# A convolution tile of the larger token group placed ahead of the first pointwise output projection on TensorE, and the value weights stored 128 bytes further on

## The chip, the core and the metric

The kernel runs on one core of one Trainium2 chip. The metric is the device time of one execution in microseconds (us), the median of several runs; lower is better. In the profile PE is TensorE (PEld its weight loads), DVE is VectorE, ACT is ScalarE, POOL is GpSimd and SP is the engine that issues the DMAs. Each engine takes its instructions in the order in which they stand in the program.

## What is computed

One step of a two-layer streaming encoder over 640 tokens (512 of a prompt, 8 streams of 16 new frames) with 1024 features, all in float32. Layer 0 is a convolution module, layer 1 is attention over a shared K/V; each is followed by a SwiGLU feed-forward net (FFN) with 2816 hidden features.

```python
def conv_module(h, hist, g, w_pw1, b_pw1, w_dw, b_dw, ln_g, ln_b, w_pw2, b_pw2):
    a, gate = jnp.split(rms_norm(h, g) @ w_pw1 + b_pw1, 2, axis=-1)
    glu = a * jax.nn.sigmoid(gate)
    full = jnp.concatenate([hist.astype(glu.dtype), glu], axis=1)
    y = lax.conv_general_dilated(full, w_dw[:, None, :], ...) + b_dw   # causal, per feature, width 31
    y = jax.nn.silu(layer_norm(y, ln_g, ln_b))
    return h + y @ w_pw2 + b_pw2, full[:, -CONV_HIST:]

h = swiglu_ffn(h, norm_ffn[l], w_ffn_in[l], w_ffn_out[l])          # after each layer
k, v = jnp.split(rms_norm(h, norm_kv) @ w_kv, 2, axis=-1)          # once, for layer 1
```

## The kernel before, in words

Features lie on the 128 partitions in 8 chunks (c = 0 to 7), tokens along the free dimension. The tokens are cut in two groups: group 0 has 256, group 1, the larger, has 384.

**Products.** Each float32 product is made of three matmuls on split operands: a weight tile `raw` is loaded by SP, ACT copies its high part to `whi` (line 156), and DVE, POOL or both write the rest to `wlo` (line 160; with `pool=3` DVE does the first quarter of the columns and POOL the other three). `whi` and `wlo` have two buffers each, so the weights after next can be split only when PE has made its last matmul with the older ones. Activations are split in the same way into `x` (high part by ACT, line 165, low part by DVE, line 166). Lines 176 to 178 are the three matmuls: high times high, low weight times high, high weight times low activation.

**The first stage.** The string `PLAN` lists its steps in program order, each with a group and chunks. Those that matter here:

- `b7`, `b5`, `b6`: the pointwise input projection (`pw1`) of chunk 7, 5 or 6 for group 1, 48 matmuls of 384 columns, then the gate (ACT lines 386 and 389, DVE line 401), which fills the chunk's row of `gp`.
- the depthwise convolution of a chunk is done on one of three engines. `d145` does chunks 4 and 5 of group 1 on DVE (lines 440 and 443, one instruction per tap and chunk); `q16` does one on ACT and POOL; `l13` and `p13` do chunk 3 of group 1 on PE. `l13` loads: POOL builds the diagonal weights (`w`, line 450) and SP copies the chunk to DRAM and back in four shifted pieces (`sc` and `x`, lines 458 and 461). `p13` is 32 matmuls (line 475; a profile shows each as two records), and ACT writes the result to `y` (line 477).
- `n0`, `n1`: the layer norm of the convolution's result. Sums by POOL (`acc`, line 201) and PE (line 210), DVE and POOL make the factor (lines 232 and 236), PE spreads it over the partitions (line 222), DVE multiplies (line 495), ACT applies the Silu (line 497), and the result is split into `x`.
- `w0`: the pointwise output projection (`pw2`) of group 0, with four weights, two outputs of 24 matmuls each; DVE adds each output to `h` (line 512).
- `r0`: the RMS norm ahead of the FFN for group 0: squares by ACT, sums by POOL and PE (line 210), factor (lines 232 and 236), spread (line 222), DVE multiplies (line 249), and a split into `x`.
- `f`: a part of the FFN of group 0. Each of its first six weights (f0 to f5 below) gives two outputs (48 matmuls of 256 columns), then follow the output weights.

The instructions are not run in plain program order: a scheduler lays them out for each engine by priority and by when it expects their inputs (splits of weights and the gates come with a raised priority, DVE's convolution fills in between), and this order is then fixed.

**The attention stage.** `proj_v` makes the values. There the split weights are the moving operand of 256 columns and the activations the stationary one: 4 weight tiles, 5 token tiles each, 24 matmuls per token tile, 480 in all.

Of the kernel before, what the change touches and what calls it, by code (L numbers as in the profile page):

```python
# [9 lines left out]
F32R = mybir.dt.float32r  # L10
# [58 lines left out]
FIN = ((4, 0), (3, 0), (2, 0), (4, 1), (1, 0), (3, 1), (0, 0), (2, 1), (1, 1), (0, 1))  # L69
SSQ1 = 'ppapappp'  # L70
LNO = ((1, 5, 4, 3, 6, 0, 2, 7), (3, 5, 6, 4, 2, 7, 1, 0))
PLAN = ("a0 y a1 a2 a4 x a3 a5 a6 l04 p04 l05 d0213 a7 b0 p05 b1 l07 p07 l06 b2 q00 s0 p06 n0 b3 b4 b5 d145 l13 w0 b7 r0 p13 b6 f q16 s1 d101 d127 n1 f f w1 r1")

V_NCONV, V_BPW1, V_BDW, V_LNG, V_LNB, V_BPW2 = 0, 8, 24, 32, 40, 48
V_NKV, V_NATT, V_NFFN, V_NFIN, V_N = 56, 64, 72, 88, 96
# [4 lines left out]
def tile_trunk(ctx, tc, xT, vecs, hist, w_pw1, w_pw2, w_in0, w_out0, w_in1, w_out1,  # L80
# [48 lines left out]
    def col(base, i):  # L129
        return vec[:, base + i:base + i + 1]  # L130

    def wsplit(src, k, n, parts=1, pool=0, cuts=1, gains=None):
        third[0] += 1
        pool3, tag = (third[1], "rx") if third[1] and third[0] % 3 == 0 else (wp, "raw")
        raw = pool3.tile([P, 2048], F32, tag=tag, name=nm(tag))
        hi = wp.tile([P, 2048], F32R, tag="whi", name=nm("whi"))
        lo = wp.tile([P, 2048], F32R, tag="wlo", name=nm("wlo"))
        sz = k * n
        if parts > 1:
            nc.sync.dma_start(raw[:, :sz].rearrange("p (m c) -> p m c", m=parts), src)  # L140
        else:
            src = src if len(src.shape) == 2 else src.rearrange("p m c -> p (m c)")
            for i in range(cuts):
                a, b = sz * i // cuts, sz * (i + 1) // cuts
                nc.sync.dma_start(raw[:, a:b], src[:, a:b])
        if gains is not None:
            for a, b, gain in gains:
                nc.scalar.activation(out=hi[:, a:b], in_=raw[:, a:b], func=AF.Copy, scale=gain)
                nc.vector.scalar_tensor_tensor(out=lo[:, a:b], in0=raw[:, a:b], scalar=gain,
                                               in1=hi[:, a:b].bitcast(F32), op0=ALU.mult,  # L150
                                               op1=ALU.subtract)
            return hi, lo
        with tc.high_priority(offset=HP):
            for i in range(cuts):
                a, b = sz * i // cuts, sz * (i + 1) // cuts
                nc.scalar.activation(out=hi[:, a:b], in_=raw[:, a:b], func=AF.Copy)  # L156
                c = b - (b - a) * pool // 4
                for eng, a, b in ((nc.vector, a, c), (nc.gpsimd, c, b)):
                    if a < b:
                        eng.tensor_tensor(out=lo[:, a:b], in0=raw[:, a:b],  # L160
                                          in1=hi[:, a:b].bitcast(F32), op=ALU.subtract)
        return hi, lo
# [517 lines left out]
        yield  # L680

    def proj_v(r):
        wh, wl = wsplit(w_v[r], 8, 256, gains=GV)
        VT = ap.tile([P, 5, 256], F32, tag="vt", name=nm("vt"), bufs=2)
        vts[r] = VT
        for tt in range(5):
            g = 0 if tt < 2 else 1
            c0 = tt * P - GR[g][0]
            pt = mmt()
            mm3(pt[:, :256], [(xs[g][0][:, k, c0:c0 + P], xs[g][1][:, k, c0:c0 + P])  # L690
                              for k in range(KT)],
                [(wh[:, k * 256:(k + 1) * 256], wl[:, k * 256:(k + 1) * 256])
                 for k in range(KT)])
# [289 lines left out]
    class Unit:  # L983
# [3 lines left out]
        def prep(u, a22=None):  # L987
            r = wp.tile([P, 2048], F32, tag="raw", name=nm("raw"))
            nc.sync.dma_start(r, w_in1[u.j])
            hi = wp.tile([P, 2048], F32R, tag="whi", name=nm("whi"))  # L990
            lo = wp.tile([P, 2048], F32R, tag="wlo", name=nm("wlo"))
            if a22 is None:
                bk = wf.tile([P, 2 * 1536], F32R, tag="bk", name=nm("bk"))
                a22 = bk[:, 0:512], bk[:, 1536:2048]
            else:
                bk = None
            q = u.q = [r[:, 512 * i:512 * i + 512] for i in range(4)]
            u.r = r[:, 0:1024]
            with tc.high_priority(offset=HP):
                xsplit(r[:, 0:1024], hi[:, 0:1024], lo[:, 0:1024])  # L1000
                xsplit(q[2], *a22)
                add(WE[0], q[0], q[0], q[3], ALU.subtract)
                add(WE[1], q[3], q[3], q[2])
                add(WE[2], q[2], q[2], q[0], ALU.subtract)
                xsplit(r[:, 1024:2048], hi[:, 1024:2048], lo[:, 1024:2048])
                add(WE[3], q[1], q[1], q[2], ALU.subtract)
            u.a11, u.a12, u.s2, u.s1 = [quarter(hi, lo, i) for i in range(4)]
            u.a22 = a22
            if bk is not None:
                u.prep_back(bk)  # L1010
# [303 lines left out]
```

## Time and profile before

| | |
|---|---|
| median of 3 runs | 1542.07 us (1539.40 to 1546.59) |
| the profiled execution | 1544.49 us |
| its span in the trace | 1542.7 us |
| share of the span that PE is busy | 95% |
| DVE, ACT, POOL | 68%, 43%, 29% |

The page of the profile sums busy times by engine and by group of instructions. Views of the trace give the instructions in order of time (start, duration, and in brackets the idle time of the engine just before, with what ended it), the waits summed by pair, and windows with each engine's busy time and the clock that PE was granted (PEclk, 1.00 is full speed). Merged instructions show a total and a count.

### The profile page before, as it was taken

What the parts mean: (1) busy time and instruction counts of PE and PEld (TensorE: products, weight loads), DVE (VectorE), ACT (ScalarE), POOL (GpSimd) and SP (SyncE); (2) the same over time, 40 slices, a digit from 0 to 9 for tenths busy, and PEclk for the clock granted to TensorE, in tenths of its full rate; (3) what the DMA queues carried; (4) which work ended last, traced back from release to release, by engine and by line L of the source; (5) the groups of instructions that cost most, each with busy time, mean ns of one, the idle gap of its engine ahead of it and who ended that gap; (6) DMA issues with size and microseconds to landing.
All of it is one profiled execution on the core that took longest, in us unless ns stands there. A gap on an engine that the chain in (4) does not pass through costs nothing.

```text
span 1542.7 us, 27212 instructions
## 1 busy us (share of the span) xinstructions
PE 1468.0 (95%) x11054; PEld 1394.8 (90%) x11054; DVE 1046.3 (68%) x1890; ACT 667.1 (43%) x1196; POOL 448.0 (29%) x406
## 2 busy tenths in 40 slices
PE   5989899989999999999999999998999999999998
PEld 5868888888999999999988798886989999999998
DVE  6994999989545455456576767666796466467456
ACT  4544445545423323235454445443564144244144
POOL 6964458987401000001322111110421011011010
PEclk9989899999999999999999999998999999999999
DMA  7874334454421333433655545444103222222222
GB/s 260 248 211 152 110 113 164 147 183 154 147 83 56 123 123 123 137 112 104 206 175 201 178 137 201 149 156 137 31 25 117 76 83 89 76 83 89 76 83 83
DMA packets 57022, 200.54 MB, mean 130 GB/s; under 512 B 10176, under 2 KB 20672, under 8 KB 44096
## 3 DMA queue, kind: packets, MB, share of 16 engines
q1 hardware_dynamic: 56608, 198.48, 38.9%
q8 instruction: 87, 1.43, 0.4%
q10 hardware_dynamic: 288, 0.31, 0.1%
q14 instruction: 39, 0.32, 0.1%
HBM read 187.55 MB, written 11.22 MB: 129 GB/s over the span
## 4 chain that ended last, share of the span: by engine, by line
PE 74%; DVE 15%; ACT 3%; issue 3%; POOL 3%; DMA 2%; SPq 0%; POOLq 0%; ACTq 0%; DVEq 0%
PE mm L177 13%; PE mm L176 13%; PE mm L178 13%; PE pb L977 6%; DVE w L443 4%; PE pc L977 4%; DVE wlo L160 4%; PE pa L977 3%; PE pb L176 1%; PE pb L178 1%; PE pb L177 1%; PE w L803 1%; PE pa L178 1%; PE pa L176 1%; PE pa L177 1%
## 5 line engine op out<-in xcount | busy, mean ns | idle before, releaser
L177 PE MATMUL mm<-x,wlo 128*128 128x256 f32 (+1 forms) x1344 | 416.5, 312 | 15.8 <-DVE wlo L160 15.3
L176 PE MATMUL mm<-x,whi 128*128 128x256 f32 (+1 forms) x1344 | 413.5, 312 | 8.8 <-ACT x L165 6.8
L178 PE MATMUL mm<-x,whi 128*128 128x256 f32 (+1 forms) x1344 | 411.2, 310 | 2.9 <-DVE x L166 2.9
L177 PEld LDWEIGHTS mm<-x,wlo 128*128 128x128 f32 x1344 | 256.2, 191 | 19.8 <-DVE wlo L160 18.5
L176 PEld LDWEIGHTS mm<-x,whi 128*128 128x128 f32 x1344 | 254.2, 191 | 13.8 <-ACT x L165 7.7
L178 PEld LDWEIGHTS mm<-x,whi 128*128 128x128 f32 x1344 | 253.8, 190 | 5.5 <-DVE x L166 4.3
L156 ACT ACTIVATE whi<-raw 128x2048 fp32r<-128x2048 f32 (+2 forms) x87 | 143.8, 1658 | 171.2 <-PE mm L178 104.7
L160 DVE TENSOR_TENSOR wlo<-raw,whi 128x2048 fp32r<-128x2048 f32 (+5 forms) x87 | 156.0, 1797 | 44.7 <-ACT whi L156 44.0
L922 POOL TENSOR_TENSOR raw<-raw 128x512 f32<-128x512 f32 x38 | 56.4, 1485 | 327.1 <-DVE raw L922 255.8
L177 PE MATMUL mm<-hid,wlo 128*128 128x256 f32 (+1 forms) x352 | 107.6, 308 | 6.0 <-DVE wlo L160 6.0
L160 POOL TENSOR_TENSOR wlo<-raw,whi 128x1536 fp32r<-128x1536 f32 (+3 forms) x33 | 93.1, 2824 | 55.4 <-ACT whi L156 55.3
L178 PE MATMUL mm<-hid,whi 128*128 128x256 f32 (+1 forms) x352 | 105.8, 307 | 0.8 <-DVE hid L166 0.7
L443 DVE SCALAR_TENSOR_TENSOR w<-gp,dwv,w 128x384 f32<-128x384 f32 x180 | 104.2, 612 | 0.9
L176 PE MATMUL mm<-hid,whi 128*128 128x256 f32 (+1 forms) x352 | 104.4, 307 | 0.0
L201 POOL TENSOR_TENSOR acc<-sq,sq 128x384 f32<-128x384 f32 (+1 forms) x8 | 8.1, 1007 | 259.1 <-ACT sq L185 259.0
L156 ACT ACTIVATE whi<-rx 128x2048 fp32r<-128x2048 f32 (+1 forms) x30 | 54.0, 1800 | 53.5 <-PE mm L178 41.5
L177 PEld LDWEIGHTS mm<-hid,wlo 128*128 128x128 f32 x352 | 66.0, 188 | 7.0 <-DVE wlo L160 7.0
L160 DVE TENSOR_TENSOR wlo<-rx,whi 128x2048 fp32r<-128x2048 f32 (+4 forms) x30 | 61.1, 2038 | 13.3 <-ACT whi L156 12.4
L423 POOL TENSOR_TENSOR y<-y,cvt 128x256 f32<-128x256 f32 (+1 forms) x60 | 68.0, 1134 | 4.3 <-ACT cvt L422 2.2
L178 PEld LDWEIGHTS mm<-hid,whi 128*128 128x128 f32 x352 | 65.7, 188 | 1.2 <-DVE hid L166 1.2
L176 PEld LDWEIGHTS mm<-hid,whi 128*128 128x128 f32 x352 | 65.1, 188 | 0.2 <-ACT hid L165 0.2
L165 ACT ACTIVATE whi<-raw 128x1024 fp32r<-128x1024 f32 x38 | 39.4, 1055 | 54.8 <-DVE raw L922 19.1
(329 smaller groups left out, 3648.2 us busy)
## 6 DMA issues: line engine op xcount, KB each, us to landing
raw<-in_w_in SPq DMA_DIRECT2D x49, 1024.0 KB
raw<-in_w_out SPq DMA_DIRECT2D x28, 768.0 KB
cache<-in_ck SPq DMA_DIRECT2D x32, 512.0 KB
cache<-in_cv SPq DMA_DIRECT2D x32, 512.0 KB
raw<-in_w_pw SPq DMA_DIRECT2D x14, 1024.0 KB
rx<-in_w_in SPq DMA_DIRECT2D x13, 1024.0 KB
rx<-in_w_pw SPq DMA_DIRECT2D x8, 1024.0 KB
raw<-in_w_kq SPq DMA_DIRECT2D x8, 1024.0 KB
```

The lines of the kernel that those rows point to most:

```text
L156: nc.scalar.activation(out=hi[:, a:b], in_=raw[:, a:b], func=AF.Copy)
L160: eng.tensor_tensor(out=lo[:, a:b], in0=raw[:, a:b], in1=hi[:, a:b].bitcast(F32), op=ALU.subtract)
L165: nc.scalar.activation(out=hi, in_=src, func=AF.Copy)
L176: nc.tensor.matmul(ps, wh, xh, start=(i == 0), stop=False)
L177: nc.tensor.matmul(ps, wl, xh, start=False, stop=False)
L178: nc.tensor.matmul(ps, wh, xl, start=False, stop=(i == last))
L201: last["acc"] = eng.tensor_tensor(out=acc[:, :n], in0=prev, in1=s(), op=ALU.add)
L423: nc.gpsimd.tensor_tensor(out=y[g][:, c, :], in0=y[g][:, c, :], in1=pr[:, :n], op=ALU.add)
L443: nc.vector.scalar_tensor_tensor(out=dst, in0=src, scalar=wj, in1=dst, op0=ALU.mult, op1=ALU.add)
L803: nc.tensor.matmul(st[32 * b:32 * b + 32, 0:512], qv[b], KC[b // 2][:, b % 2, :], start=True, stop=True)
L922: ENG[e].tensor_tensor(out=out, in0=a, in1=b, op=op)
L977: nc.tensor.matmul(ps, a[:, c], b[:, k, :], start=(first and k == 0 and i == 0), stop=(k == 3 and i == 2), skip_group_check=not first)
```

## The change

Two edits. In `PLAN`, `l13` moves from behind `d145` to behind `b4`, and `p13` from behind `r0` to behind `d145`, that is ahead of `w0`, `b7` and `r0`. And the buffers of `whi` and `wlo` become 2112 elements wide (8448 bytes where there were 8192), of which 2048 are used: from the start everywhere, except in `proj_v`, where the weights begin 32 elements (128 bytes) in. All tiles that lie behind them in memory move by 256 to 1024 bytes, each by a multiple of 256.

```diff
-PLAN = ("a0 y a1 a2 a4 x a3 a5 a6 l04 p04 l05 d0213 a7 b0 p05 b1 l07 p07 l06 b2 q00 s0 p06 n0 b3 b4 b5 d145 l13 w0 b7 r0 p13 b6 f q16 s1 d101 d127 n1 f f w1 r1")
+PLAN = ("a0 y a1 a2 a4 x a3 a5 a6 l04 p04 l05 d0213 a7 b0 p05 b1 l07 p07 l06 b2 q00 s0 p06 n0 b3 b4 l13 b5 d145 p13 w0 b7 r0 b6 f q16 s1 d101 d127 n1 f f w1 r1")
...
-    def wsplit(src, k, n, parts=1, pool=0, cuts=1, gains=None):
+    def wsplit(src, k, n, parts=1, pool=0, cuts=1, gains=None, off=0):
...
-        hi = wp.tile([P, 2048], F32R, tag="whi", name=nm("whi"))
-        lo = wp.tile([P, 2048], F32R, tag="wlo", name=nm("wlo"))
+        hi = wp.tile([P, 2112], F32R, tag="whi", name=nm("whi"))[:, off:off + 2048]
+        lo = wp.tile([P, 2112], F32R, tag="wlo", name=nm("wlo"))[:, off:off + 2048]
...
-        wh, wl = wsplit(w_v[r], 8, 256, gains=GV)
+        wh, wl = wsplit(w_v[r], 8, 256, gains=GV, off=32)
...
-            hi = wp.tile([P, 2048], F32R, tag="whi", name=nm("whi"))
-            lo = wp.tile([P, 2048], F32R, tag="wlo", name=nm("wlo"))
+            hi = wp.tile([P, 2112], F32R, tag="whi", name=nm("whi"))[:, 0:2048]
+            lo = wp.tile([P, 2112], F32R, tag="wlo", name=nm("wlo"))[:, 0:2048]
```

SP's order of DMAs is the same in both programs, and POOL builds the weights of the tile at the same place: the loads of `l13` do not move. What moves is shown at two places, on PE and on DVE. The numbers in names count tiles.

**Ahead of w0.** PE before, from the last matmul of `b5` (`mm_1601`) over the sum and the spread of `n0` to the first two outputs of `w0` (`mm_1712`, `mm_1738`):

```order
L178 MATMUL mm_1601<-x_502,whi_1571 128x384
L210 MATMUL w_171_1373<-onec,acc_1376 128x1 x2
L222 MATMUL w_171_1373<-ident,rst_182_1402 128x128 x2
L176 MATMUL mm_1712<-x_1406,whi_1706 128x256
L177 MATMUL mm_1712<-x_1406,wlo_1707 128x256
L176 MATMUL mm_1738<-x_1406,whi_1706 128x256
```

PE now, where the last of `b5` is `mm_1610` and the first outputs of `w0` are `mm_1746` and `mm_1772`:

```order
L178 MATMUL mm_1610<-x_502,whi_1580 128x384
L475 MATMUL mm_1705<-x_208_1574,w_206_1570 32x384 x15
L210 MATMUL w_171_1373<-onec,acc_1376 128x1 x2
L475 MATMUL mm_1705<-x_208_1574,w_206_1570 32x384 x17
L222 MATMUL w_171_1373<-ident,rst_182_1402 128x128 x2
L176 MATMUL mm_1746<-x_1406,whi_1740 128x256
L177 MATMUL mm_1746<-x_1406,wlo_1741 128x256
L176 MATMUL mm_1772<-x_1406,whi_1740 128x256
```

The 32 matmuls of `p13` now stand around the sum of `n0`. On DVE at the same place before, from the split of the first weight of `w0` (`wlo_1707`) to the multiplication of `n0` (line 495):

```order
L160 TENSOR_TENSOR wlo_1707<-rx_1705,whi_1706 128x1024
L440 TENSOR_SCALAR w_213_1631<-gp,dwv,vec 128x384
L401 SCALAR_TENSOR_TENSOR gp<-t_211_1626,t_212_1628 128x384
L232 TENSOR_SCALAR rst_1400<-w_171_1373 128x2
L440 TENSOR_SCALAR w_213_1631<-gp,dwv,vec 128x384
L443 SCALAR_TENSOR_TENSOR w_213_1631<-gp,dwv,w_213_1631 128x384
L160 TENSOR_TENSOR wlo_1766<-raw_1764,whi_1765 128x1024
L443 SCALAR_TENSOR_TENSOR w_213_1631<-gp,dwv,w_213_1631 128x384
L495 TENSOR_TENSOR y_109<-y_109,w_171_1373 128x256 x8
```

And now, with the first weight of `w0` in `wlo_1741` and the second in `wlo_1800`:

```order
L160 TENSOR_TENSOR wlo_1741<-rx_1739,whi_1740 128x1024
L440 TENSOR_SCALAR w_216_1640<-gp,dwv,vec 128x384
L401 SCALAR_TENSOR_TENSOR gp<-t_214_1635,t_215_1637 128x384
L440 TENSOR_SCALAR w_216_1640<-gp,dwv,vec 128x384
L443 SCALAR_TENSOR_TENSOR w_216_1640<-gp,dwv,w_216_1640 128x384
L160 TENSOR_TENSOR wlo_1800<-raw_1798,whi_1799 128x1024
L443 SCALAR_TENSOR_TENSOR w_216_1640<-gp,dwv,w_216_1640 128x384
L232 TENSOR_SCALAR rst_1400<-w_171_1373 128x2
L443 SCALAR_TENSOR_TENSOR w_216_1640<-gp,dwv,w_216_1640 128x384 x4
L495 TENSOR_TENSOR y_109<-y_109,w_171_1373 128x256 x8
```

The step of the factor (line 232) now stands behind the second weight's split, and five convolution instructions rather than one stand between that split and line 495.

**Ahead of the FFN.** PE before, from the end of `b7` (`mm_1973`) over the sum and spread of `r0` and all of `b6` (`mm_2109`, `mm_2134`) to the first output of f0 (`mm_2172`):

```order
L178 MATMUL mm_1973<-x_502,whi_1942 128x384
L210 MATMUL w_244_2003<-onec,acc_2006 128x1 x2
L475 MATMUL mm_2069<-x_216_1700,w_214_1696 32x384 x20
L222 MATMUL w_244_2003<-ident,rst_255_2032 128x128 x2
L475 MATMUL mm_2069<-x_216_1700,w_214_1696 32x384 x12
L176 MATMUL mm_2109<-x_502,whi_2104 128x384
...
L178 MATMUL mm_2134<-x_502,whi_2104 128x384
L176 MATMUL mm_2172<-x_2036,whi_2166 128x256
```

PE now, with the end of `b7` in `mm_2007`:

```order
L178 MATMUL mm_2007<-x_502,whi_1976 128x384
L210 MATMUL w_245_2037<-onec,acc_2040 128x1 x2
L176 MATMUL mm_2109<-x_502,whi_2104 128x384
...
L176 MATMUL mm_2134<-x_502,whi_2104 128x384
L222 MATMUL w_245_2037<-ident,rst_256_2066 128x128 x2
L177 MATMUL mm_2134<-x_502,wlo_2105 128x384
...
L178 MATMUL mm_2134<-x_502,whi_2104 128x384
L176 MATMUL mm_2172<-x_2070,whi_2166 128x256
```

Half of `b6` now covers the factor of `r0`, and the other half is what is left between the spread and f0. On DVE before, the last of the eight multiplications of `r0` (`n_264`), the last low parts of its `x`, and the split of f1's weight (`wlo_2230`):

```order
L249 SCALAR_TENSOR_TENSOR n_264_2065<-h,vec,w_244_2003 128x256
L166 TENSOR_TENSOR x_2036<-n_263_2061,x_2036 128x256
L443 SCALAR_TENSOR_TENSOR w_213_1631<-gp,dwv,w_213_1631 128x384
L440 TENSOR_SCALAR w_366_2823<-gp,dwv,vec 128x384
L166 TENSOR_TENSOR x_2036<-n_264_2065,x_2036 128x256
L443 SCALAR_TENSOR_TENSOR w_213_1631<-gp,dwv,w_213_1631 128x384
L401 SCALAR_TENSOR_TENSOR gp<-t_271_2159,t_272_2161 128x384
L440 TENSOR_SCALAR w_366_2823<-gp,dwv,vec 128x384
L443 SCALAR_TENSOR_TENSOR w_213_1631<-gp,dwv,w_213_1631 128x384
L160 TENSOR_TENSOR wlo_2230<-raw_2228,whi_2229 128x512
```

Now, from the fourth of the eight multiplications (`n_261`) to the low part of the sixth:

```order
L249 SCALAR_TENSOR_TENSOR n_261_2083<-h,vec,w_245_2037 128x256
L443 SCALAR_TENSOR_TENSOR w_216_1640<-gp,dwv,w_216_1640 128x384
L166 TENSOR_TENSOR x_2070<-n_260_2079,x_2070 128x256
L443 SCALAR_TENSOR_TENSOR w_216_1640<-gp,dwv,w_216_1640 128x384
L401 SCALAR_TENSOR_TENSOR gp<-t_271_2159,t_272_2161 128x384
L249 SCALAR_TENSOR_TENSOR n_262_2087<-h,vec,w_245_2037 128x256
L443 SCALAR_TENSOR_TENSOR w_216_1640<-gp,dwv,w_216_1640 128x384
L160 TENSOR_TENSOR wlo_2230<-raw_2228,whi_2229 128x512
L166 TENSOR_TENSOR x_2070<-n_261_2083,x_2070 128x256
L443 SCALAR_TENSOR_TENSOR w_216_1640<-gp,dwv,w_216_1640 128x384
L249 SCALAR_TENSOR_TENSOR n_263_2091<-h,vec,w_245_2037 128x256
```

The split of f1's weight, the gate of `b6` (line 401) and two more convolution instructions now stand among the eight parts of `x`, four of which come after that split.

Two things follow in PE's order. The first four outputs of `w0` (96 matmuls) are interleaved in both programs; the first weight's last matmul is the 68th of them before and the 81st now. And where f0's two outputs came one after the other (48 matmuls) and f1's behind them, the four are now interleaved part by part of `x`: f0's weight has its last matmul as the 94th of the 96. The sums of `n1` (line 210) stand 78 matmuls earlier on PE than before.

## The prediction

> **What bounds the kernel now.** First the page: its head, the busy times and the chain that ended last.
>
> ```profile
> span 1542.7 us, 27212 instructions
> PE 1468.0 (95%) x11054; PEld 1394.8 (90%) x11054; DVE 1046.3 (68%) x1890; ACT 667.1 (43%) x1196; POOL 448.0 (29%) x406
> PE 74%; DVE 15%; ACT 3%; issue 3%; POOL 3%; DMA 2%; SPq 0%; POOLq 0%; ACTq 0%; DVEq 0%
> ```
>
> PE is busy for 95% of the span and makes 74% of the chain. So a change pays where it takes idle time or slow clock from PE, and costs where it adds them. The waits of PE, summed over the span, show where that is:
>
> ```profile
> PE mm L177 <- DVE wlo L160: 21.3, 18, 2.5
> ...
> PE mm L176 <- ACT x L165: 6.8, 3, 5.1
> ```
>
> The largest sum is the wait for split weights (18 times, at most 2.5 us). Of the wait for `x`, 5.1 us are one wait, and PE in order of time shows that it is the one ahead of w0:
>
> ```profile
> 149.78 0.34 PE L178 MATMUL mm<-x,whi 128*128 128x384 f32 x1
> 150.92 0.61 PE L210 MATMUL w<-onec,acc 128*128 128x1 f32 x4 [0.81 <-POOL acc L201]
> 152.56 0.71 PE L222 MATMUL w<-ident,rst 128*128 128x128 f32 x4 [1.04 <-POOL rst L236]
> 158.37 0.58 PE L176 MATMUL mm<-x,whi 128*128 128x256 f32 x1 [5.09 <-ACT x L165]
> ```
>
> From 150.1 to 158.4 PE does only the sum and the spread of n0. Windows over the same stretch (the columns I use are PE's busy time with its matmuls, and PEclk) show a second price:
>
> ```profile
> 149.90:154.30 4.40, 1.53 (x10) 1.04 (x8) 3.26 (x5) 3.66 (x3) 3.29 (x4) 1.00 0.45 188
> 154.30:158.40 4.10, 0.03 (x1) 0.03 (x1) 4.10 (x8) 1.48 (x4) 0.65 (x1) 0.50 0.30 64
> 158.40:164.50 6.10, 6.10 (x28) 6.10 (x29) 6.06 (x16) 4.34 (x11) 0.00 (x0) 0.50 0.32 132
> 164.50:172.80 8.30, 8.30 (x72) 8.25 (x70) 7.56 (x15) 3.85 (x6) 1.35 (x1) 1.00 0.00 0
> ```
>
> At 154.3 the clock falls to half and stays there until 164.5. The 28 matmuls of 158.4 to 164.5 took 6.1 us; at the rate of the next row (72 in 8.3 us, 0.115 each) they would take 3.2. So the slow clock costs 2.9 us behind a gap of 8.3.
>
> The other place is ahead of the FFN, where p13 stands now:
>
> ```profile
> 193.94 0.34 PE L178 MATMUL mm<-x,whi 128*128 128x384 f32 x1
> 194.11 0.50 PE L210 MATMUL w<-onec,acc 128*128 128x1 f32 x4
> 194.54 3.43 PE L475 MATMUL mm<-x,w 128*32 128x384 f32 x40
> 197.90 0.71 PE L222 MATMUL w<-ident,rst 128*128 128x128 f32 x4
> 198.54 2.14 PE L475 MATMUL mm<-x,w 128*32 128x384 f32 x24
> 200.62 0.45 PE L176 MATMUL mm<-x,whi 128*128 128x384 f32 x1
> ```
>
> There is no idle time in it: p13's 3.43 + 2.14 = 5.57 us hide the factor of r0, and with b6 behind it the making of x. b6 is 48 matmuls of 384 columns, at 1.5 x 0.115 = 0.173 each 8.3 us: 200.6 to 208.9.
>
> **Part 1: p13 ahead of w0.** Its inputs are there: SP issues the four reads of its pieces from 135.38 (row below), and POOL and SP keep their order. So it starts at 150.1. What sets w0's start is DVE:
>
> ```profile
> 135.38 1.75 SPq L461 DMA_DIRECT2D x<-sc  x4
> 151.56 0.16 DVE L232 TENSOR_SCALAR rst<-w 128x2 f32<-128x2 f32 x1 [0.24 <-PE w L210]
> 152.88 3.15 DVE L160 TENSOR_TENSOR wlo<-raw,whi 128x1024 fp32r<-128x1024 f32 x1
> 156.48 2.72 DVE L495 TENSOR_TENSOR y<-y,w 128x256 f32<-128x256 f32 x8
> L443 DVE SCALAR_TENSOR_TENSOR w<-gp,dwv,w 128x384 f32<-128x384 f32 x180 | 104.2, 612 | 0.9
> ```
>
> Line 232 now follows the split: that ends near 155.8, then one L443 (0.6), so line 232 runs at about 156.3 and not 151.6. POOL's power (0.71 in the trace) and the spread bring it to about 157.9. DVE meanwhile does four L443 (2.4) and takes up line 495 at about 158.5, 2.0 later than the 156.48 of before. So w0 starts near 160.4 with p13 behind it: 5.57 of work moved in for 2.0 of delay. Nothing else on PE is held up, since ACT, which is busy for 1.00 of the 4.40 and 0.50 of the 4.10 us in the windows above, empties p13's PSUM buffer long before w0 comes to it.
>
> **Part 2: the clock at w0.** p13 ends near 155.9. What stays idle is 1.3 to the spread, and 2.5 behind it. The nearest rows on both sides:
>
> ```profile
> 174.96 0.38 PE L177 MATMUL mm<-x,wlo 128*128 128x256 f32 x1 [2.01 <-DVE wlo L160]
> 174.90:182.90 8.00, 7.94 (x69) 7.94 (x70) 7.89 (x13) 3.45 (x5) 6.53 (x6) 1.00 0.76 257
> 218.30 0.39 PE L177 MATMUL mm<-x,wlo 128*128 128x256 f32 x1 [2.52 <-DVE wlo L160]
> 219.20:222.60 3.40, 3.40 (x18) 3.40 (x17) 3.40 (x8) 1.43 (x3) 3.40 (x2) 0.51 0.89 272
> ```
>
> A wait of 2.01 left the clock at 1.00, one of 2.52 was followed by 3.4 us at half. Mine of 1.3 and 2.5 is at the second: I give half a chance to each. On PE the first weight of w0 is also used for 13 matmuls longer (the 81st, not the 68th), which puts off the next split by 13 x 0.115 = 1.5. At b7's end that makes +2.0 + 1.5 = +3.5 with a slow clock as before, and with the 2.9 gained and about 0.5 of waiting for x, +1.1; the middle is +2.3. The Trainium skill, "TensorE: Matmul & The Clock Gate", Part 1, says that the clock falls after an idle window of about 3.4 us, and sets gaps below that as harmless. By it neither piece would slow w0, and the sum would be 1.2 lower; the row at 219.2 speaks against it.
>
> **Part 3: ahead of the FFN.** b7 ends at 194.1 + 2.3 = 196.4. With the sum (0.5), b6 (8.3) and the spread (0.7), PE comes to f0 at about 205.9, 3.0 ahead of the 208.9 of before. But x is made by DVE, and p13 no longer covers it:
>
> ```profile
> 202.54 0.86 DVE L249 SCALAR_TENSOR_TENSOR n<-h,vec,w 128x256 f32<-128x256 f32 x2
> 212.81 0.41 DVE L166 TENSOR_TENSOR x<-n,x 128x256 fp32r<-128x256 f32 x1
> 215.24 3.01 DVE L160 TENSOR_TENSOR wlo<-raw,whi 128x512 fp32r<-128x512 f32 x1
> ```
>
> DVE hardly idles between w0 and here, so I start its row at 203.0 (one L443 more than before). To the 10.7 us that the eight parts took are added f1's split (3.0), two L443 (1.2) and the gate (0.5): the last part comes at about 218.4. PE has 96 interleaved matmuls to make against these parts; the last 20 or so wait for the end and finish near 220.7. Before, f1's matmuls ended at 225.2, so PE leads by 4.5. This lead is lost at f2. Its weight goes into f0's buffer, which is free at 220.7 where it was free at 215.3, and the refill takes these steps:
>
> ```profile
> 215.38 0.40 PE L176 MATMUL mm<-x,whi 128*128 128x256 f32 x2
> 216.14 1.90 ACT L156 ACTIVATE whi<-raw 128x2048 fp32r<-128x2048 f32 x1
> 220.16 3.48 POOL L160 TENSOR_TENSOR wlo<-raw,whi 128x1536 fp32r<-128x1536 f32 x1
> 225.26 0.39 PE L176 MATMUL mm<-x,whi 128*128 128x256 f32 x2
> 225.49 0.28 PE L177 MATMUL mm<-x,wlo 128*128 128x256 f32 x1
> ```
>
> 0.8 from PE's last matmul to ACT, 1.9 for ACT, then DVE's quarter beside POOL (3.0, like f1's): 220.7 + 5.7 = 226.4, against the 225.49 at which f2's matmuls flow now. That is +0.9.
>
> **Part 4: the clock in the FFN.** PE waits there twice: about 4.5 us for f1's split, mostly hidden since x sets the pace (+0.7, bounds 0 and 2), and the 5.7 us ahead of f2, like the gap ahead of w0. What follows is half speed for 3.4 to 6.1 us of work, 1.7 to 2.9 lost; I take +2.0. After f3 the new program is at 0.9 + 0.7 + 2.0 = +3.6.
>
> **Part 5: what comes back.** DVE has made four convolution instructions more by line 495 and two more among the parts of x: 6 x 0.6 = 3.6 us that no longer stand ahead of weight splits in the FFN. PE's waits for those splits shorten by something between 0 and 3.6; -1.0, nearer to none, because POOL's 3.48 ends most of them.
>
> **Part 6: the value weights.** Moving weights of 256 columns are read in the attention stage and in the last FFN. By shape:
>
> ```profile
> L177 PE MATMUL mm<-whi,x 128*128 128x256 f32 x160 | 45.1, 282 | 0.0
> L177 PE MATMUL pa<-whi,hc 128*128 128x256 f32 x144 | 40.0, 277 | 0.0
> ```
>
> One takes 282 ns in proj_v, 277 at the end. If the place in memory makes the difference, the shift gains 480 (160 of each of the three kinds) x 4.5 ns = 2.2; if not, nothing. I take -0.9. The Trainium skill, "SBUF — State Buffer", in the section on the DMA port swizzle, says that the memory is read in lines of 16 bytes and only a crossing without a second hit costs. 128 bytes are eight whole lines, so by it the gain is 0 and the sum 0.9 higher; no run here shows it yet.
>
> The sum: +3.6 - 1.0 - 0.9 = +1.7 us. The profiled execution took 1544.49 (1.8 outside its span), so 1546.2; it was 2.4 over the median of 1542.07, and on the median the forecast is **1543.8 us**. A difference under 0.5% (7.7 us) is about what a measurement of this kernel can't tell from none: I forecast no change.
>
> **The rivals.** (a) *The gap is filled and nothing comes due later*: the FFN's x keeps up, PE saves 5.57 and the 2.9 of slow clock, 8.5 in all: 1533.6. For it: the gap is there, the work fits into it. Against it: DVE is the engine that makes x, and in the windows above it was busy for 6.06 of 6.10 us and 7.89 of 8.00. Chance 0.08. (b) *Slower: PE's clock*. Three shorter gaps take the place of one, and each is followed by half speed: +1.2 at w0, +1.3 and +0.9 in the FFN on top of Part 4, nothing returned (1.9), and the sums of n1, which the order now puts 78 matmuls (9.0 us at 0.115) earlier on PE, wait about 2 for the convolution: 1.7 + 7.3 = +9.0, 1551.1. It decides from waits of about 2.5 us on. Chance 0.08. The row for n1's sums: POOL has its last part ready at 336.8 and PE asks for it at 340.0.
>
> ```profile
> 333.30 3.46 POOL L201 TENSOR_TENSOR acc<-acc,y 128x384 f32<-128x384 f32 x3 [0.15 <-ACT y L446]
> 339.97 0.72 PE L210 MATMUL w<-onec,acc 128*128 128x1 f32 x6
> ```
>
> (c) *Neither edit does anything*: p13's time comes back exactly ahead of the FFN and the shift is without effect, 1542.1. It lies inside my range; chance 0.20.
>
> **How the numbers follow.** My forecast has 0.64, (a) 0.08, (b) 0.08, (c) 0.20. Faster by over 0.5% is (a), 0.08; slower is (b), 0.08; within 0.5% are the others, 0.84. The range: downwards the clock stays full at w0 (-1.2), Part 4 costs 0.7 and not 2.7 (-2.0), Part 5 gives 2.5 (-1.5), Part 6 gives 2.2 (-1.3), and the waits for x at w0 and f0 hide wholly (-0.5 and -0.7): -7.2, so 1536.6. Upwards +6.2 of (b)'s 7.3, to 1550.0.
>
> **What would show it.** Right: line 475 between 150 and 156 with 64 records, w0's first matmul at about 160, the last part of x near 218 with f1's split among the parts, f2's stall on `wlo` near 221 to 226, and half clock behind it. The prediction is wrong if f2's matmuls flow before 224 or after 230, if PEclk is 1.00 throughout 155 to 235, or if proj_v's records stay at 282 with a time that is still lower by several us.

## The result, and the profile after

The changed kernel took 1562.74 us (median of 4 runs, 1560.68 to 1566.69), the kernel before 1544.33 us (4 runs, 1539.40 to 1546.78) beside it: ratio 1.013, 95% interval 1.0111 to 1.0148, so 1.3% or some 20 us slower. The forecast was no change, 1536.6 to 1550.0 us: the prediction was wrong. One run of e8_pool0_before (below) was slow from end to end, 2084.38 us at 0.65 of the clock, and is left out of that kernel's figure.

The page of the changed kernel, the lines that answer to those shown of before:

```profile
span 1558.9 us, 27215 instructions
PE 1476.1 (95%) x11054; PEld 1403.6 (90%) x11054; DVE 1060.9 (68%) x1890; ACT 667.9 (43%) x1196; POOL 448.2 (29%) x406
PE 73%; DVE 15%; DMA 3%; POOL 3%; ACT 3%; issue 3%; SPq 0%; POOLq 0%; ACTq 0%; DVEq 0%
```

The counts are those of before, but DVE is busy for 1060.9 us and not 1046.3: 14.6 us more for the same 1890 instructions. The groups by shape say which. First before, then after (the last columns are the count, busy us and mean ns, then idle time ahead):

```profile
L160 DVE TENSOR_TENSOR wlo<-raw,whi 128x512 fp32r<-128x512 f32 x16 | 20.9, 1316 | 3.0 <-ACT whi L156 3.0
L160 DVE TENSOR_TENSOR wlo<-rx,whi 128x512 fp32r<-128x512 f32 x7 | 15.9, 2278 | 0.0
L443 DVE SCALAR_TENSOR_TENSOR w<-gp,dwv,w 128x384 f32<-128x384 f32 x180 | 104.2, 612 | 0.9
```

```profile
L160 DVE TENSOR_TENSOR wlo<-raw,whi 128x512 fp32r<-128x512 f32 x16 | 33.7, 2115 | 2.2 <-ACT whi L156 2.2
L160 DVE TENSOR_TENSOR wlo<-rx,whi 128x512 fp32r<-128x512 f32 x7 | 19.8, 2824 | 2.6 <-ACT whi L156 1.6 <-POOL acc L201 1.1
L443 DVE SCALAR_TENSOR_TENSOR w<-gp,dwv,w 128x384 f32<-128x384 f32 x180 | 104.1, 613 | 0.9
```

The 23 subtractions of 512 columns take 53.5 us, before 36.8. Five of them stand ahead of 106 us and did not change; the other 18 are the quarters of the FFN's weight splits that VectorE makes while GpSimd makes three. The convolution did not change. PE's summed waits show who pays:

```profile
PE mm L177 <- DVE wlo L160: 29.0, 19, 3.6
PE mm L176 <- ACT x L165: 4.8, 4, 2.6
PE mm L176 <- ACT whi L156: 4.6, 5, 1.9
PE w L222 <- DVE mst L486: 1.7, 1, 1.7
```

The wait for split weights grew from 21.3 to 29.0 us. Ahead of w0 the change did what it says. PE in order of time:

```profile
149.56 2.78 PE L475 MATMUL mm<-x,w 128*32 128x384 f32 x30
152.28 0.61 PE L210 MATMUL w<-onec,acc 128*128 128x1 f32 x4
152.81 3.41 PE L475 MATMUL mm<-x,w 128*32 128x384 f32 x34
156.31 0.71 PE L222 MATMUL w<-ident,rst 128*128 128x128 f32 x4
159.61 0.58 PE L176 MATMUL mm<-x,whi 128*128 128x256 f32 x1 [2.58 <-ACT x L165]
```

The tile fills the gap, and w0 starts 1.24 us later than before (159.61 for 158.37). The loss is at the other end, in the FFN's first stretch. PE, DVE and POOL there:

```profile
215.54 0.58 PE L177 MATMUL mm<-x,wlo 128*128 128x256 f32 x1 [3.04 <-DVE wlo L160]
228.28 0.50 PE L176 MATMUL mm<-x,whi 128*128 128x256 f32 x2 [1.92 <-ACT whi L156]
232.35 0.58 PE L177 MATMUL mm<-x,wlo 128*128 128x256 f32 x1 [3.57 <-DVE wlo L160]
```

```profile
205.71 0.87 DVE L249 SCALAR_TENSOR_TENSOR n<-h,vec,w 128x256 f32<-128x256 f32 x2
...
211.77 3.71 DVE L160 TENSOR_TENSOR wlo<-raw,whi 128x512 fp32r<-128x512 f32 x1
215.41 1.22 DVE L166 TENSOR_TENSOR x<-n,x 128x256 fp32r<-128x256 f32 x1
...
222.51 0.71 DVE L166 TENSOR_TENSOR x<-n,x 128x256 fp32r<-128x256 f32 x1
...
228.37 3.92 DVE L160 TENSOR_TENSOR wlo<-raw,whi 128x512 fp32r<-128x512 f32 x1
...
342.00 0.69 DVE L160 TENSOR_TENSOR wlo<-raw,whi 128x512 fp32r<-128x512 f32 x1 [0.72 <-ACT whi L156]
```

```profile
211.49 3.44 POOL L160 TENSOR_TENSOR wlo<-raw,whi 128x1536 fp32r<-128x1536 f32 x1 [8.08 <-ACT whi L156]
...
228.30 3.44 POOL L160 TENSOR_TENSOR wlo<-raw,whi 128x1536 fp32r<-128x1536 f32 x1 [2.02 <-ACT whi L156]
```

The quarter at 342.00, with no subtraction of GpSimd's beside it, takes 0.69. The one at 211.77 takes 3.71: GpSimd's began 0.28 earlier and ended at 214.93, and VectorE's ended 0.55 later, about its own length. VectorE stood still for some 3 us, in its row of parts of x, four of which stand behind. At 228.37 it happened again. The windows of the same stretch, after and then before (PEclk is the third number from the end):

```profile
215.00:225.00 10.00, 9.46 (x62) 9.46 (x63) 10.00 (x19) 4.01 (x8) 6.43 (x6) 0.74 0.34 107
225.00:235.00 10.00, 4.51 (x26) 4.11 (x25) 9.97 (x11) 6.75 (x10) 7.90 (x4) 0.77 0.18 42
235.00:245.00 10.00, 9.48 (x63) 9.19 (x62) 10.00 (x19) 2.56 (x4) 6.17 (x6) 0.72 0.40 143
```

```profile
215.00:225.00 10.00, 7.48 (x51) 7.28 (x50) 10.00 (x13) 4.85 (x8) 9.92 (x5) 0.83 0.42 117
225.00:235.00 10.00, 9.42 (x82) 9.22 (x81) 10.00 (x16) 6.27 (x8) 8.61 (x6) 1.00 0.51 177
235.00:245.00 10.00, 8.69 (x74) 8.28 (x73) 9.96 (x17) 6.43 (x10) 9.19 (x6) 1.00 0.26 87
```

Thirty microseconds hold 151 matmuls and not 207, with waits and half clock in turn.

To see where time comes and goes, the same matmul (counted from the program's end, since the order there is one) is looked up in both traces. How much later than before, in us, at the time of before in the head (the runs are those below; for the first two columns the matmuls around f2 differ a little in order):

| trace | 225.7 | 237.6 | 300.0 | 330.1 | 345.0 | 382.8 | 440.1 | 738.5 | 1535.0 |
|---|---|---|---|---|---|---|---|---|---|
| changed | 7.2 | 10.0 | 14.7 | 13.1 | 19.3 | 20.5 | 21.7 | 21.8 | 16.4 |
| e1_plan | 6.7 | 7.4 | 9.5 | 7.9 | 16.7 | 18.1 | 19.0 | 19.0 | 19.0 |
| e2_offset | -1.7 | -1.7 | 0.0 | 0.1 | 0.1 | 0.1 | 0.3 | 0.5 | -4.7 |
| e3_tile | 6.9 | 10.1 | 15.1 | 13.4 | 22.4 | 23.9 | 25.3 | 25.3 | 24.2 |
| e6_warm | 7.7 | 6.3 | 9.6 | 13.2 | 13.2 | 13.3 | 13.8 | 14.0 | 8.3 |
| e7_pool0 | -0.2 | 0.8 | 3.4 | 2.2 | 2.7 | -0.4 | 18.5 | 18.7 | 17.0 |
| e8_pool0_before | -5.9 | -2.9 | 2.2 | 0.9 | 0.8 | -0.8 | 20.8 | 21.0 | 17.1 |
| e9_twice | 1.2 | 0.7 | 3.8 | 4.7 | 6.3 | 6.3 | 6.6 | 6.6 | 1.7 |
| e11_three | 1.9 | 2.1 | 5.9 | 4.8 | 6.2 | 4.5 | 10.2 | 10.3 | 7.8 |
| e13_three_before | -2.4 | -3.4 | 1.4 | 0.2 | 1.0 | -0.1 | 7.3 | 7.3 | 2.9 |
| e14_three_warm | 3.9 | 3.0 | 6.4 | 5.1 | 5.1 | 5.1 | 5.5 | 5.8 | 4.2 |

All of the loss is there by 440, half of it by 237.6. e2_offset, whose order is that of before, shows that two traces differ by up to 1.7 us in the first columns for other reasons than the order. The step between 330 and 345 stands at n1: PE waits there three times where it did not wait before, 3.4 us for two of VectorE's quarters and 1.7 us for VectorE's copy of three numbers per partition (line 486) ahead of the spread. The copy before, after, and GpSimd after:

```profile
341.83 0.17 DVE L486 COPY mst<-mst 128x3 f32<-128x3 f32 x1
```

```profile
347.63 3.23 DVE L486 COPY mst<-mst 128x3 f32<-128x3 f32 x1
```

```profile
346.93 3.90 POOL L160 TENSOR_TENSOR wlo<-rx,whi 128x1536 fp32r<-128x1536 f32 x1
```

It took 3.23 us for 0.17 of work, and ended with GpSimd's split (350.83). The 3 to 5 us that some of the traces win between 738.5 and 1535 are mostly no effect of the edits. Of these, 3.2 to 3.6 are won between 1069 and 1080 us of the trace of before, in the attention stage. PE's waits there are about 1 us long at most, and yet the clock behind them is at half for 10.2 us in some executions (that of before is one) and full in others. Before, and the changed kernel:

```profile
1069.00:1080.00 11.00, 9.40 (x66) 5.00 (x66) 2.29 (x9) 1.79 (x6) 0.00 (x0) 0.53 0.28 96
```

```profile
1086.00:1097.00 11.00, 7.43 (x109) 4.23 (x108) 5.05 (x11) 3.39 (x8) 0.00 (x0) 1.00 0.28 98
```

So the medians are compared, and the table only up to 738.5.

### The profile page after: what moved, and what is told of

It is laid out like the page before. It is cut to its first block, busy times and chain, and to the rows that moved or that the text cites. A ratio compares the mean times of both kernels' runs of the same rounds, so it can differ in the third digit from the quotient of the medians.

```text
span 1558.9 us, 27215 instructions
## 1 busy us (share of the span) xinstructions
PE 1476.1 (95%) x11054; PEld 1403.6 (90%) x11054; DVE 1060.9 (68%) x1890; ACT 667.9 (43%) x1196; POOL 448.2 (29%) x406
## 4 chain that ended last, share of the span: by engine, by line
PE 73%; DVE 15%; DMA 3%; POOL 3%; ACT 3%; issue 3%; SPq 0%; POOLq 0%; ACTq 0%; DVEq 0%
PE mm L177 13%; PE mm L176 13%; PE mm L178 13%; PE pb L977 6%; DVE wlo L160 4%; PE pc L977 4%; DVE w L443 4%; PE pa L977 4%; PE pb L176 1%; PE pb L178 1%; PE pb L177 1%; PE w L803 1%; PE pa L178 1%; PE pa L176 1%; PE pa L177 1%
## 5 line engine op out<-in xcount | busy, mean ns | idle before, releaser
L177 PE MATMUL mm<-x,wlo 128*128 128x256 f32 (+1 forms) x1344 | 421.0, 315 | 21.9 <-DVE wlo L160 21.2
L176 PE MATMUL mm<-x,whi 128*128 128x256 f32 (+1 forms) x1344 | 418.4, 316 | 10.2 <-ACT x L165 4.8
L178 PE MATMUL mm<-x,whi 128*128 128x256 f32 (+1 forms) x1344 | 414.7, 313 | 2.4 <-DVE x L166 2.3
L177 PEld LDWEIGHTS mm<-x,wlo 128*128 128x128 f32 x1344 | 259.8, 193 | 25.8 <-DVE wlo L160 24.8
L176 PEld LDWEIGHTS mm<-x,whi 128*128 128x128 f32 x1344 | 258.3, 194 | 15.4 <-ACT x L165 5.9
L178 PEld LDWEIGHTS mm<-x,whi 128*128 128x128 f32 x1344 | 257.4, 193 | 5.2 <-DVE x L166 4.2
L160 DVE TENSOR_TENSOR wlo<-raw,whi 128x2048 fp32r<-128x2048 f32 (+5 forms) x87 | 167.4, 1928 | 45.6 <-ACT whi L156 45.6
L443 DVE SCALAR_TENSOR_TENSOR w<-gp,dwv,w 128x384 f32<-128x384 f32 x180 | 104.1, 613 | 0.9
L160 DVE TENSOR_TENSOR wlo<-rx,whi 128x2048 fp32r<-128x2048 f32 (+4 forms) x30 | 66.3, 2208 | 14.9 <-ACT whi L156 13.8
```

The source lines that it names most:

```text
L160: eng.tensor_tensor(out=lo[:, a:b], in0=raw[:, a:b], in1=hi[:, a:b].bitcast(F32), op=ALU.subtract)
L176: nc.tensor.matmul(ps, wh, xh, start=(i == 0), stop=False)
L177: nc.tensor.matmul(ps, wl, xh, start=False, stop=False)
L178: nc.tensor.matmul(ps, wh, xl, start=False, stop=(i == last))
L443: nc.vector.scalar_tensor_tensor(out=dst, in0=src, scalar=wj, in1=dst, op0=ALU.mult, op1=ALU.add)
```

## The experiments

**Which edit.** Theory O says that the order costs, rival M the memory. e1_plan is the kernel before with

```
-... b3 b4 b5 d145 l13 w0 b7 r0 p13 b6 f ...
+... b3 b4 l13 b5 d145 p13 w0 b7 r0 b6 f ...
```

> Theory O (the order): the loss comes from the new order alone, through VectorE, which the profile of before has at 100% from 200 to 300 us and which now stands longer in splits and products that run beside GpSimd; then this run, with the moved tile and without the shift of the value weights, is 18 to 21 us over the kernel before. Rival M (the memory): the 256 to 512 bytes by which the weight buffers moved make VectorE's subtractions slower (the group of 512 columns went from 1316 to 2115 ns); then this run is only 2 to 5 us over the kernel before, and that group is back near 1316.

1562.48 us against 1542.66: ratio 1.0126 (1.0105 to 1.0147). e2_offset has the old order and the rest of the diff (buffers of 2112 columns, off=32 for the value weights):

> The old order with the larger weight buffers and the value weights 128 bytes further on. Theory O: 0.5 to 2 us under the kernel before, all of it in the attention stage (the 480 matmuls with value weights at 277 to 280 instead of 282 ns). Rival M: 13 to 18 us over the kernel before, with VectorE's split of 512 columns near 2100 ns.

1540.26 against 1542.66: 0.9979 (0.9962 to 0.9996). The quarters tell the same: 1942 ns in e1_plan, 1315 in e2_offset.

```profile
L160 DVE TENSOR_TENSOR wlo<-raw,whi 128x512 fp32r<-128x512 f32 x16 | 30.9, 1942 | 2.4 <-ACT whi L156 2.4
```

```profile
L160 DVE TENSOR_TENSOR wlo<-raw,whi 128x512 fp32r<-128x512 f32 x16 | 20.9, 1315 | 3.0 <-ACT whi L156 3.0
```

M is out. In e2_offset the mean time from one matmul's start to the next among those with value weights is 115.4 ns, before 117.1 (445 intervals of each trace): 480 x 1.7 = 0.8 us. What its median shows beyond that may be chance: its interval reaches from 0.6 to 5.9 us, and 3.5 us of the gain in its trace are the clock at 1069.

**Which half of the order.** e3_tile moves p13 alone, e4_loads l13 alone.

```
-... b4 b5 d145 l13 w0 b7 r0 p13 b6 f ...
+... b4 b5 d145 l13 p13 w0 b7 r0 b6 f ...     (e3_tile)
+... b4 l13 b5 d145 w0 b7 r0 p13 b6 f ...     (e4_loads)
```

> Only the 64 matmuls of the tile are moved (p13); its loads (l13) stay where they were, buffers as before. VectorE's order around the FFN is that of the changed kernel. Theory O: 18 to 21 us over the kernel before. Rival L (the earlier loads, with the weights' product on GpSimd ahead of b5, are what costs): within 4 us of the kernel before.

> Only the loads are moved (l13 ahead of b5), the 64 matmuls stay behind r0. VectorE's order around the FFN is that of the kernel before. Theory O: within 1.5 us of the kernel before. Rival L: 13 us or more over it.

e3_tile 1567.07 against 1542.66, 1.0153 (1.0132 to 1.0174), a little more than expected; e4_loads 1540.84, 0.9985 (0.9965 to 1.0005). The 64 moved matmuls make the loss, the loads none of it.

**Missing behind r0, or harmful ahead of w0.** Three kernels ask this. e9_twice makes the tile in both places, e10_between puts it between w0 and b7, e5_cover lets another tile take the place behind r0 and takes that channel from VectorE:

```
-... b4 l13 b5 d145 p13 w0 b7 r0 b6 f q16 s1 d101 d127 ...
+... b4 l13 b5 d145 p13 w0 b7 r0 p13 b6 f q16 s1 d101 d127 ...       (e9_twice)
+... b4 l13 b5 d145 w0 p13 b7 r0 b6 f q16 s1 d101 d127 ...           (e10_between)
+... b4 l13 b5 d145 p13 l12 w0 b7 r0 p12 b6 f q16 s1 d101 d17 ...    (e5_cover)
```

> The changed kernel with the tile's 64 matmuls made a second time behind r0 (the same result, written again; VectorE's work is that of the changed kernel). VectorE's order has f1's split behind all eight parts of x again. Theory O (what is missing behind r0 costs, through the order that follows from it): although TensorE has 5.6 us more to do, the time is 1543 to 1550. Rival W (the later start of w0 and of all that follows on VectorE costs, 2.8 us at r0's factor, and grows from there): 1558 or more.

> The tile between w0 and b7: the stretch ahead of w0 is that of the kernel before, and r0 has no cover but b6. Theory O: 12 us or more over the kernel before. Rival W: within 4 us of it, since nothing is later at w0.

> The changed kernel with a second tile of the larger group on TensorE (channel 2, loads behind the first tile, its 64 matmuls behind r0 where the first one stood); VectorE makes that channel's convolution no more (29 + 1 instructions of 0.61 to 0.67 us, 18.5 us less). With the cover back, VectorE's order has f1's split behind all eight parts of x again. Theory O (the loss comes from what stands behind r0 without cover): f2's matmuls flow at or before 227 us, and the time is 1530 to 1543. Rival W (the tile ahead of w0 is itself what costs): 1553 or more.

e9_twice took 1548.08 against 1541.44: 1.004 (1.0026 to 1.0055). With 5.6 us more on TensorE it is 0.9% faster than the changed kernel. In its trace f1's split is behind the parts of x, and f1's matmuls flow at 219.53 (before 218.30):

```profile
213.26 0.75 DVE L166 TENSOR_TENSOR x<-n,x 128x256 fp32r<-128x256 f32 x2
...
216.55 2.92 DVE L160 TENSOR_TENSOR wlo<-raw,whi 128x512 fp32r<-128x512 f32 x1
```

```profile
219.53 0.46 PE L177 MATMUL mm<-x,wlo 128*128 128x256 f32 x1 [2.01 <-DVE wlo L160]
```

e10_between took 1554.77: 1.0079 (1.0054 to 1.0104). Nothing stands ahead of w0 there, and it loses 12 us, at the low end of what O expected: again f1's split is among the parts of x, and f2 flows at 230.44.

```profile
212.11 3.38 DVE L160 TENSOR_TENSOR wlo<-raw,whi 128x512 fp32r<-128x512 f32 x1
215.41 1.22 DVE L166 TENSOR_TENSOR x<-n,x 128x256 fp32r<-128x256 f32 x1
```

```profile
215.54 0.58 PE L177 MATMUL mm<-x,wlo 128*128 128x256 f32 x1 [3.03 <-DVE wlo L160]
...
230.44 0.58 PE L177 MATMUL mm<-x,wlo 128*128 128x256 f32 x1 [3.56 <-DVE wlo L160]
```

e5_cover took 1546.94 against 1540.62: 1.0029 (1.0013 to 1.0046). In its trace f2's matmuls come 0.1 us later than before, as O has it, but the time is a miss: I expected 1530 to 1543, because VectorE makes one channel less. That is 31 instructions, not the 30 that I counted, and line 443 is busy for 88.0 us where it was 104.1. Yet the time is only 0.1% from e9_twice, where VectorE makes all of it. So rival W is out, and so is the thought that each microsecond of VectorE's work counts. That the moment of its splits counts is what the next runs test.

**The standing still and the slow clock.** e6_warm fills the two long waits with matmuls that are thrown away, in ffn_in:

```
+for _ in range(WARM.get((j, ab), 0) if g == 0 else 0):   # {(1, 1): 20, (2, 1): 26}
+    nc.tensor.matmul(pt[:, :n], wh[:, ab*1024:ab*1024+P], xs[g][0][:, 0, :], start=True, stop=True)
```

> The changed kernel with the first matmul of f1's second output made 20 times more and that of f2's second output 26 times more (5.4 us of TensorE work inside the two long waits for split weights; each output starts afresh behind them). Theory C (the slow clock behind these waits is a loss of its own, 6.6 us by the windows from 187 to 247): the clock stays full from 213 to 245 and the time is 4 to 7 us under the changed kernel's 1562.7. Rival V (VectorE sets the pace in this stretch, so TensorE only waits longer): within 2 us of 1562.7.

1553.73 against 1540.62: 1.0087 (1.006 to 1.0114), 0.43% or 6.6 us under the changed kernel's 1.013. Theory C held in size, but the clock was only better and not full:

```profile
215.00:225.00 10.00, 10.00 (x79) 9.54 (x77) 10.00 (x17) 3.40 (x7) 6.51 (x6) 0.95 0.32 105
225.00:235.00 10.00, 8.31 (x56) 7.91 (x55) 9.96 (x15) 7.76 (x12) 9.21 (x6) 0.83 0.19 60
235.00:245.00 10.00, 9.24 (x82) 9.04 (x80) 10.00 (x17) 4.56 (x7) 9.13 (x6) 1.00 0.37 125
```

f2 flows no earlier, but f3 ends 6.3 and not 10.0 us late. The agreement in size is in part luck: by the table 3.7 us are won at f3, none of it is left at 330.1, and 6 to 8 us are won from n1 on, where no wait was filled.

e7_pool0 and e8_pool0_before set the share of GpSimd in the first three FFN chunks' splits to nothing (PFA = 3 becomes 0), in the changed kernel and in the one before:

> The changed kernel, with GpSimd's three quarters of the weight splits of the first three FFN chunks (30 splits) given to VectorE. Theory P (VectorE's subtractions stand still while GpSimd's of 3.4 us runs, 2.1 to 2.8 us for a quarter that takes about 0.6 alone): the whole split takes 2.2 to 2.4 us on VectorE, less than the wait and the quarter together, products with the low part drop to 0.42 each, and the time is 8 to 20 us under the changed kernel's. Rival V (VectorE is full, so each us given to it is added): 15 us or more over the changed kernel's.

> The same edit made to the kernel before. Theory P: 0 to 10 us under the kernel before (its quarters took 1.3 to 2.3 us, so there is less to win than in the changed kernel). Rival V: 15 us or more over it.

e7_pool0 1559.20, 1.0115 (1.008 to 1.0149); e8_pool0_before 1561.48, 1.0137 (1.0108 to 1.0167). On the kernel before V came true, on the changed one neither did: the same edit costs 21 us there and nothing that shows here. So where GpSimd has no share in these splits, the new order is no slower than the old one. The traces show why the sum misleads: up to 382.8 neither had lost anything (table). Then in e7_pool0

```profile
395.75 1.44 PE L210 MATMUL w<-onec,acc 128*128 128x1 f32 x6 [10.71 <-POOL acc L201]
```

These are n1's second sums, those of the squares. They wait 10.71 us because VectorE had put off the convolution for its splits: its last instruction ends at 366.0, in the trace of before at 332.6, and all of n1 hangs on it. e8_pool0_before has the same wait, 12.17 us. So the FFN's loss goes when the standing still goes, and a second bill comes at n1 in either order.

e11_three gives VectorE only f1's, f2's and f3's splits whole, and e13_three_before does so in the kernel before:

```
-        wh, wl = wsplit(wsrc[j], 16, P, pool=pool)
+        wh, wl = wsplit(wsrc[j], 16, P, pool=pool if j not in (1, 2, 3) else 0)
```

> The changed kernel, with VectorE alone splitting the weights of f1, f2 and f3 (GpSimd makes none of these three; the 27 others as before). Theory P (VectorE stands still beside GpSimd's 3.4 us in these three, 3.7, 3.9 and 3.1 us for a quarter): each whole split takes 2.2 to 2.4 us, f2's matmuls flow by 229 instead of 232.4, and the time is 3 to 9 us under the changed kernel's. Rival V: 3 x 1.7 us more of VectorE's work, 2 to 6 us over the changed kernel's.

> The kernel before, with VectorE alone splitting the weights of f1, f2 and f3, as in the run on the changed kernel that gave back some 9 us. There VectorE's quarters stood 3.7, 3.9 and 3.1 us beside GpSimd; here 3.0, 2.0 and 2.8. Theory P (the standing still is part of what the new order costs): the gain is smaller, 0 to 5 us. If it is 9 us here too, the edit helps whatever the order and says nothing of the cause. Rival V: 2 to 5 us over the kernel before.

e11_three took 1551.83 against 1541.44: 1.0069 (1.0044 to 1.0095), 0.6% or 9 us under the changed kernel. e13_three_before took 1546.12 against 1541.25: 1.0041 (1.0025 to 1.0056), 5 to 6 us over its own, so there theory P missed (it had 0 to 5 under) and V came true. One edit, two signs: what it takes away is in the new order and not in the old. With the edit in both, the orders differ by 0.28%, some 4 us by the medians, where they differed by 20. In e11_three the whole split takes less time than the quarter did, and f2 flows at 227.00:

```profile
210.06 2.28 DVE L160 TENSOR_TENSOR wlo<-raw,whi 128x2048 fp32r<-128x2048 f32 x1
...
224.67 2.28 DVE L160 TENSOR_TENSOR wlo<-raw,whi 128x2048 fp32r<-128x2048 f32 x1
```

```profile
227.00 0.58 PE L177 MATMUL mm<-x,wlo 128*128 128x256 f32 x1 [2.13 <-DVE wlo L160]
```

e14_three_warm has both repairs (13 and 17 thrown-away matmuls):

> The changed kernel with both edits: VectorE alone splits f1 to f3, and TensorE repeats the first matmul of f1's second output 13 times and that of f2's second output 17 times in its waits. If the standing still and the slow clock are two costs that add, the time is 12 to 16 us under the changed kernel's, 3 to 7 over the kernel before. If both took away the same microseconds, it is within 2 us of the run with the three splits alone (0.7% over the kernel before).

1551.44 against 1541.25: 1.0059 (1.0037 to 1.0082), 0.1% from e11_three. By the medians the two repairs mend the same microseconds, which fits a slow clock that only follows the long waits.

**A version without the harm.** e12_parts keeps the loads and the shift, with the tile in its old place:

> What of the change did no harm, together: the earlier loads and the shifted value weights, with the tile where the kernel before has it. From the sums of their own runs (0.9979 and 0.9985): 2 to 4 us under the kernel before if both are real; within 1.5 us of it if the loads did nothing (their interval holds 1).

1540.62 against 1541.44, 0.9989 (0.9975 to 1.0003): no difference that these runs show. e2_offset is the only kernel whose interval lies under 1.

## Why the prediction was wrong, step by step

**Part 1 and 2, ahead of w0: the times were right, the path in part by luck.** Forecast: w0 near 160.4, waits of 1.3 and 2.5 us, b7's end at 196.4. Measured: 159.61, a wait of 2.58 ahead of it and none ahead of the spread, and r0's sum at 197.26, so +3.2 where I took +2.3 and gave 3.5 as the bound. Half clock followed, for 6.8 us. I had w0's start set by VectorE, with line 232 at 156.3 behind a split of 3.15 us. The split took 1.22 and line 232 stood at 153.79; it was the spread, behind the tile's last matmul on TensorE, for which VectorE then waited (0.55 us, at 157.06).

At 440 us the sum stood at +2.6 (Parts 1 to 5) and the trace at +21.7. Of these 19 us, 6.4 were missed in Parts 3 and 4, up to f3's end, and 12.7 in Part 5. By the runs without GpSimd's share (e7_pool0, e8_pool0_before) most of both has one root: what VectorE's splits cost beside GpSimd's.

**Part 3: the step that failed is the row of x.** "I start its row at 203.0 ... the last part comes at about 218.4": it started at 205.71 and its last part ended at 223.2. Of the 4.8 us, 2.7 are the start (b7's end came 0.9 later than forecast, and VectorE was not as full at w0 as I said: it waited 2.58 us for w0's first output at 172.0, where it had waited 0.51). The other 2.1 are the row: 17.5 us for 15.4, since f1's quarter took 3.71 and not 3.0, and the eight low parts took 4.8 and not 3.1 us. I had read 3.01 off the trace of before as the quarter's price, but it was the price of that moment; alone it is 0.69. f1's matmuls had a wait of 3.04 that I took to be hidden and half clock behind it, and were done at 226.4 instead of 220.7. From there the refill took 6.0 us and not 5.7. So f2 flowed at 232.35, 6.9 us late where the sum said +0.9, and past the 230 that I had named as a sign of being wrong. That I saw this wait come is right; its size was off by 6.

**Part 4: mis-sized.** 2.7 us were set down for the clock and one wait. Between b7 and f3 TensorE is busy at half clock for 12.4 us now and for 3.4 before. Half of that is lost, 6.2 and 1.7 us, so 4.5 for the clock alone. At f3's end the change stood at +10.0, not +3.6.

**Part 5: the wrong sign, and the largest miss.** It said -1.0: fewer convolutions ahead of the later splits. In fact another 11.7 us were lost between 237.6 and 440. VectorE now came to its quarters more often when GpSimd's three quarters had just begun: the last four took 3.7 to 4.0 us each, where three of the last four before took 1.2 or less, the 23 together 53.5 and not 36.8, and n1's copy 3.23 and not 0.17. That these make up the 11.7 us fits e7_pool0 and e8_pool0_before, which have lost nothing by 382.8 in either order. What an instruction of VectorE's costs beside GpSimd had to be bounded from both sides, 0.69 to about 4.0; I took the old prices for given, and so the range ended at 1550.0.

The Trainium skill, "SBUF — State Buffer", "Who interferes with whom", states this: a VectorE instruction with two inputs in SBUF, or a copy in a two-port mode, and a GpSimd instruction that reads SBUF exclude each other: the one that came second waits until the first is done. The trace agrees: the quarter 0.69 to 3.71, the copy 0.17 to 3.23 (in which mode it ran no run shows), while line 443, with one of its two tensors in PSUM, stays at 612 and 613 ns. At 337.42 in the trace of before VectorE's quarter began 0.04 us ahead of GpSimd's part: it took 0.69, and GpSimd's 3.98 where 3.5 is common. The prediction named this page for 16-byte lines and not for this.

**Part 6: right in size.** -0.9 was taken; the intervals between matmuls give 0.8. The test that I set for it was not a good one: I looked for records that leave 282 ns, and they went to 281. The interval from start to start shows the gain, the duration hardly.

**The rivals.** (b) had the right sign and a part of the mechanism, the clock behind short waits, but priced it at 9 us, and n1's sums, which it made wait for the convolution, did not wait in the changed kernel (only in e7_pool0 and e8_pool0_before). (a) is answered by e9_twice: a tile more in the gap ahead of w0 costs 6.2 us (4 to 8.5), as much as its own 5.6 of TensorE's time. At f2 it had cost 1.2 of these; the rest came due by 345 us. So filling that gap gained nothing that lasts, even with the cover behind r0 kept. (c) is out too: far more than the tile's own time came due.

**What stays open.** By the medians some 9 of the 20 us remain in e14_three_warm (the three whole splits alone cost 5 to 6 in the old order); its one trace has 3.9 us at f2 and 5.5 at 440. No run takes these apart, nor what the filled gap at w0 gives back to later stages. Nor does a run move f1's split alone in VectorE's order: that its place among the parts of x does the harm ahead of f2 is read from the traces of e9_twice, e10_between and the changed kernel.

## What to carry to other kernels

Work that covers a wait holds an order behind it: before moving it, ask which engine's row is exposed at the place that it leaves, and look there at the new order instruction by instruction. Price an instruction of VectorE's with two SBUF inputs by its row alone and by its row beside GpSimd, and take both ends into the range. A quarter shared with a slower engine can take longer than the whole: here 3.7 us for 512 columns beside GpSimd, 2.28 for 2048 alone; but whether that matters depends on the order (e11_three and e13_three_before).

## What the hardware showed

The wait beside GpSimd has a price by the moment. In all 16 traces VectorE's subtractions of 512 columns that began while one of GpSimd's weight splits ran, 204 in all, ended 0.54 to 0.56 us after it, so they took from 0.85 to 4.04 us. The changed kernel has 18 of them, the kernel before 15, and 3 in which VectorE came first.

The clock is set on a grid. In every trace the stretches at half speed last whole multiples of 3.413 us (3.4 to 20.5, but for the one that the end cuts off) and start at whole multiples of it from one another (changed kernel: 158.7, 213.4, 230.4, 250.9, 285.0). One and the same wait of 3.01 us, for the third of w0's weights, was followed by half clock in e1_plan and not in the changed kernel, whose order there is the same. The windows of the two, e1_plan first:

```profile
172.00:182.00 10.00, 6.78 (x35) 6.58 (x36) 7.46 (x9) 3.68 (x7) 8.76 (x5) 0.66 0.45 138
```

```profile
172.00:182.00 10.00, 6.75 (x55) 6.34 (x54) 9.71 (x14) 5.05 (x6) 7.89 (x4) 1.00 0.29 105
```

PE is busy as long, with 35 matmuls in one and 55 in the other. So a wait of 2 to 3 us has no fixed price: what it costs goes with where it falls on the grid, and that differs from run to run. In e1_plan 1.87 us of idle time fall into one piece of the grid (170.86 to 174.27); in the changed kernel a point of the grid (175.81) parts the wait, and the two pieces have 1.46 and 1.79. Between 60 and 1500 us of the 16 traces all 77 pieces at full clock with more than 1.85 us idle on PE are followed by half clock, and 45 of the other 6476, 33 of these with 1.5 to 1.85. The Trainium skill, "TensorE: Matmul & The Clock Gate", Part 1, gives the window of 3413 ns and says that it runs freely, which these lengths bear out. That it takes an idle window of about 3.4 us they don't: a wait of 2.58 us was enough at w0, and in the 3.4 us ahead of 213.4 eight matmuls start.
